# One layer on one core: a transfer of weights on ScalarE's queue placed behind a small GpSimd copy

## The chip, the cores and the metric

The kernel runs on one core of one Trainium2 chip. The metric is the device time of one execution in microseconds. The core has a matrix engine (TensorE, PE in the profile; its weight loads are PEld), a vector engine (VectorE, DVE), a scalar engine (ScalarE, ACT), GpSimd (POOL) and SyncE (SP), which only issues transfers. Transfers (DMAs) are issued by SP, ACT and POOL and moved by 16 DMA engines.

## The reference

One layer of a hybrid encoder on x of 256 rows and 2048 columns, in float32:

```
h = rms_norm(x, attn_norm)
x = x + hybrid_mixer(h, w_in, ...)      # proj = h @ w_in, two kinds of attention, then @ w_out
h = rms_norm(x, ffn_norm)
x = x + conv_ffn(h, w_up, conv_w, conv_b, w_down)
```

The projection `h @ w_in` has 6152 columns: queries, keys, values and gates of eight heads of forgetting attention, then queries, keys and values of eight heads of stick-breaking attention. The change lies in the opening, where the first 512 columns of that projection (queries of four heads) are computed and the kernel's data come in for the first time.

## The kernel before

All large products are done in two parts. A float32 operand is split into a rounded high part and a remainder (`hi`, `lo`), and three products (hi by hi, hi by lo, lo by hi) are summed in PSUM. For weights, ACT or DVE makes `hi` by a copy with a cast, and DVE makes `lo` by a subtraction. For x, TensorE transposes a block of 128 columns by a product with the identity, ACT writes `hi` (scaled by the norm's weight, `ga`), and DVE writes `lo`; both go into `hT`. The factor of the norm's root mean square is applied to the result, later.

After the opening the order is: the rest of the input projection and attention, step by step interleaved; the output projection; then the feed-forward network in parts of eight feature blocks. In those stages SP loads one 1 MB piece of weights after another, ACT and DVE split it, and TensorE multiplies.

The function `opening` (from line 383) computes the first 512 columns of the projection over the 16 blocks of x, two blocks (one "c") at a time, c from 0 to 7. Its work on PE, DVE, ACT and SP stands in the order in which it is written (`manual_schedule`); POOL's order is left to the scheduler. The pieces that matter here:

- `load_x(k, n)` (line 91): SP loads n blocks of x from block k. I call them x0, x2, x4 and so on by k.
- `load_w(c, which, queue)` (line 395): loads weights of step c, either both halves or one, on SP or on ACT. `load_w(0, 0)`, `load_w(0, 1, nc.scalar)`, `load_w(1, 0, nc.scalar)` and `load_w(1, 1)` are w00, w01, w10 and w11, 256 KB each; all four lie in one tile, w_raw.
- Lines 369 to 373: DVE clears `zeros`, POOL builds the identity in `ident` (a memset and an `affine_select`).
- `keep_busy(n)` (line 379): n products of `zeros`, whose result nobody reads. There are 14 before the first transposes and four between the transposes and the first real product.
- `columns` (line 129): TensorE turns the norm's weight from rows (`prow`) to columns (`ga`).
- `split_w(0)`: DVE casts w00 (line 407), the two blocks of x0 are transposed (139), ACT writes their `hi` (144) and DVE their `lo` (147), DVE makes w00's remainder (417); then ACT casts w01 (416) and DVE makes its remainder.
- `multiply` (line 426): four products for each half in `hi`, two in `lo`. The eight products of w00 and w01 in `hi` stand first; then, behind the preparation of step 1, the four in `lo`.
- `split_w(1)`: DVE casts w10 and w11 (line 413), the two blocks of x2 are transposed.

The start of the transfers, as written in `opening`:

```
load_x(0, 2)
nc.scalar.dma_start(prow[:KT, :], attn_norm[0].rearrange("(n p) -> n p", p=P))
act.preload_act_table_set("natural_log_exp_and_others")
load_w(0, 0)
load_w(0, 1, nc.scalar)
load_x(2, 2)
load_w(1, 0, nc.scalar)
load_w(1, 1)
load_x(4, 2)
load_w(2)
```

The layer that records the program adds the waits between engines. For transfers of SP and ACT it has eight semaphores, used in turn; a transfer that takes a semaphore again is issued only when that semaphore's former transfer has landed, and the engine that issues it waits for that.

Of the kernel before, what the change touches and what calls it, by code (L numbers as in the profile page):

```python
# [45 lines left out]
def hybrid_layer(  # L46
# [19 lines left out]
    nc = tc.nc  # L66
# [11 lines left out]
    def f32(t):  # L78
        return t.bitcast(F32)
# [10 lines left out]
    def load_x(k, n):  # L90
        nc.sync.dma_start(x2[:, :, k * P : (k + n) * P], xp[:, :, k * P : (k + n) * P])

    ident = cs[:, C_ID : C_ID + P]
# [33 lines left out]
    def columns(dst, rows, n):  # L127
        pp = psb.tile([P, 512], F32, name="pp", tag="t")
        nc.tensor.transpose(pp[:, :n], rows, ident[:n, :n])
        dve.tensor_copy(dst, pp[:, :n])  # L130
# [3 lines left out]
    def transposed_split(k, g, n=2):  # L134

        ps = psb.tile([P, 2, S], F32, name="ps_x", tag="t")
        for j in range(n):
            for t in range(NT):
                nc.tensor.transpose(
                    ps[:, j, t * P : (t + 1) * P], xt[t][:, (k + j) * P : (k + j + 1) * P], ident  # L140
                )
        for j in range(n):
            i = k + j
            act.activation(hT[:, i, 0, :], ps[:, j, :], AF.Identity, scale=g[:, i : i + 1])
        for j in range(n):
            i = k + j
            dve.scalar_tensor_tensor(
                hT[:, i, 1, :], ps[:, j, :], g[:, i : i + 1], f32(hT[:, i, 0, :]),
                op0=ALU.mult, op1=ALU.subtract,
            )  # L150

    def sums_of_squares(ss, c, tiles=range(NT)):

        for t in tiles:
            junk = late.tile([P, 512], F32, name="junk", tag="raw", bufs=4)
            act.activation(junk, xt[t][:, c * 512 : (c + 1) * 512], AF.Square, accum_out=ss[:, t, c : c + 1])
# [62 lines left out]
    def rows_of(w, k0, n, c0, cols):  # L219
        return w[k0 * P : (k0 + n) * P, c0 : c0 + cols].rearrange("(k p) c -> p k c", p=P)  # L220
# [14 lines left out]
    def of_half(h, part, t):  # L235
        return h[:, part, t * P : (t + 1) * P]
# [48 lines left out]
    with ExitStack() as actx:  # L285
# [57 lines left out]
        def attended(po, h, g, group):  # L343
# [28 lines left out]
            ident, ident, pattern=[[-1, P]], base=0, channel_multiplier=1,  # L372
# [4 lines left out]
        def keep_busy(n):  # L377
            for _ in range(n):
                nc.tensor.matmul(idle, zeros[:, :P], zeros, start=True, stop=True)
# [3 lines left out]
        def opening():  # L383

            acc = psa.tile([P, NT, 512], F32, name="acc", tag="acc")
            pairs = [[(0, 1), (1, 1)]] + [[(0, 2)]] * 7
            raws, parts = [], []

            def load_w(c, which=None, queue=nc.sync):

                if c == len(raws):
                    raw = wraw.tile([P, 2048], F32, name="w_raw", tag="w_raw")
                    raws.extend([raw[:, :1024], raw[:, 1024:]])
                for i, n in [(which, 1)] if which is not None else [(0, 2)]:
                    queue.dma_start(
                        raws[c][:, i * 512 : (i + n) * 512].rearrange("p (a b) -> p a b", a=n),
                        rows_of(wi, 2 * c + i, n, 0, 512),
                    )

            def split_w(c):  # L400
                hi = whi.tile([P, 2048], F32R, name="w_hi", tag="w_hi")
                lo = wlo.tile([P, 2048], F32R, name="w_lo", tag="w_lo")
                parts.append([t[:, :1024].rearrange("p (a b) -> p a b", a=2) for t in (hi, lo)])
                for i, n in pairs[c]:
                    cols = slice(i * 512, (i + n) * 512)
                    if c == i == 0:
                        dve.tensor_copy(hi[:, cols], raws[c][:, cols])
                        for k in range(2):
                            transposed_split(k, ga, 1)
                    elif c == 1:  # L410
                        for j in range(2):
                            half = slice(512 * j, 512 * (j + 1))
                            dve.tensor_copy(hi[:, half], raws[c][:, half])
                        transposed_split(2, ga)
                    else:
                        act.copy(hi[:, cols], raws[c][:, cols])
                    dve.tensor_tensor(
                        lo[:, cols], raws[c][:, cols], f32(hi[:, cols]), op=ALU.subtract
                    )

            def multiply(c, i, n, high):
                hi, lo = (p[:, i : i + n] for p in parts[c])
                order = [(j, l, hi) for j in range(n) for l in range(2)] if high else [(j, 0, lo) for j in range(n)]
                for m, (j, l, r) in enumerate(order):
                    for t in range(NT):
                        nc.tensor.matmul(
                            acc[:, t, :], of_half(hT[:, 2 * c + i + j], l, t), r[:, j, :],
                            start=high and c == i == m == 0, stop=not high and c == 7 and m == n - 1,
                        )

            load_x(0, 2)
            nc.scalar.dma_start(prow[:KT, :], attn_norm[0].rearrange("(n p) -> n p", p=P))
            act.preload_act_table_set("natural_log_exp_and_others")
            load_w(0, 0)
            load_w(0, 1, nc.scalar)
            load_x(2, 2)
            load_w(1, 0, nc.scalar)
# [3 lines that stand above are left out]
            load_x(6, 2)  # L441
            load_w(3)
            load_x(8, 4)
            load_w(4)
            load_x(12, 4)
            load_w(5)
            keep_busy(14)
            columns(ga, prow[:KT, :], KT)
            split_w(0)
            keep_busy(4)  # L450

            def behind(c):
                if c:
                    transposed_split(2 * c + 2, ga)
                split_w(c + 1)

            multiply(0, 0, 1, True)
            multiply(0, 1, 1, True)
            behind(0)
            sums_of_squares(ss1, 0, [0])  # L460
            multiply(0, 0, 1, False)
            multiply(0, 1, 1, False)
            for c in range(1, 8):
                if c < 7:
                    behind(c)
                sums_of_squares(ss1, c // 2, [c % 2])
                if c == 2:
                    load_w(6)
                    load_w(7)
                multiply(c, 0, 2, True)  # L470
                multiply(c, 0, 2, False)
            return acc

        with tc.high_priority(offset=AHEAD), tc.manual_schedule(
            engines={mybir.EngineType.PE, mybir.EngineType.DVE, mybir.EngineType.Activation, mybir.EngineType.SP}
        ):
            acc_q0 = opening()
# [687 lines left out]
```

## Time and profile before

| | |
|---|---|
| median of 3 runs | 1104.94 us (1104.69 to 1105.36) |
| the profiled execution | 1104.87 us |
| its span, first to last instruction | 1103.1 us |
| granted clock of TensorE | 1.000 |
| TensorE with work | 1097.9 us |
| DVE, ACT, POOL with work | 876.2, 701.6, 44.4 us |
| read from memory | 242.89 MB, 222 GB/s over the span |

A row of the timeline has the start in microseconds from the span's start, the duration, the engine, the line, the operation, out<-in, and in brackets how long the engine was idle before and what ended it. An engine's name with a q (SPq, ACTq) is its sequencer, which issues a transfer. The duration of a row with xN runs from the first of the N to the end of the last. A row of the waits has who waited for whom, microseconds in total, how often, and the longest. A row of the stretches has the stretch, its length, the busy time (and count) of PE, PEld, DVE, ACT and POOL, the granted clock, the share of the DMA engines and GB/s. Products are pipelined: the next one starts before the one before it has ended.

### The profile page before, as it was taken

How to read it: one execution, taken by the hardware profiler on the slowest of the kernel's cores; microseconds unless marked ns; L12 is line 12 of the kernel's file. 1: busy time of each engine (PE TensorE's matmuls, PEld its weight loads, DVE VectorE, ACT ScalarE, POOL GpSimd, SP SyncE). 2: the span in 40 equal slices, each digit the busy share in tenths (PEclk: the TensorE clock that was granted, in tenths of full speed). 3: DMA queues.
4: the chain of work that ended last, by engine and by line, in shares of the span. 5: the costliest groups of instructions: out<-in, count | busy, mean ns of one | idle time of the engine just before them, and what ended most of it. 6: DMA issues, size and time to landing. Idle time of an engine off the chain costs nothing. (4 is left out here: it accounts for less than half of the span.)

```text
span 1103.1 us, 14847 instructions
## 1 busy us (share of the span) xinstructions
PE 1097.9 (100%) x5872; PEld 951.4 (86%) x5872; DVE 876.2 (79%) x940; ACT 701.6 (64%) x879; POOL 44.4 (4%) x46
## 2 busy tenths in 40 slices
PE   9999999999999999999999999999999999999998
PEld 7998888888888888888888888888888888888887
DVE  5755787785775677679889988889798889889896
ACT  6543565664553567667767776767676677677753
POOL 0000000000000000000000010100000010100010
PEclk9999999999999999999999999999999999999999
DMA  8776555565555396558989597986979688987985
GB/s 290 187 230 229 189 153 160 175 217 182 184 160 187 112 318 202 188 176 208 288 225 309 191 235 263 263 268 176 318 207 308 212 219 277 247 265 196 326 210 167
DMA packets 179407, 245.96 MB, mean 223 GB/s; under 512 B 4432, under 2 KB 119018, under 8 KB 179082
## 3 DMA queue, kind: packets, MB, share of 16 engines
q1 hardware_dynamic: 162458, 209.73, 58.4%
q0 software_dynamic: 16560, 34.75, 16.6%
q8 instruction: 46, 0.75, 0.3%
q10 hardware_dynamic: 320, 0.53, 0.2%
q14 instruction: 23, 0.19, 0.0%
HBM read 242.89 MB, written 2.11 MB: 222 GB/s over the span
## 5 line engine op out<-in xcount | busy, mean ns | idle before, releaser
L209 DVE TENSOR_TENSOR w_lo<-w_raw,w_hi 128x2048 fp32r<-128x2048 f32 (+1 forms) x196 | 439.7, 2246 | 148.7 <-ACT w_hi L208 148.0
L208 ACT CAST w_hi<-w_raw 128x2048 fp32r<-128x2048 f32 (+1 forms) x196 | 367.3, 1876 | 278.6 <-PE pu L257 83.4
L257 PE MATMUL pu<-hT,w_hi 128*128 128x512 f32 x1664 | 397.1, 390 | 0.0
L257 PEld LDWEIGHTS pu<-hT,w_hi 128*128 128x128 f32 x1664 | 309.4, 188 | 62.4
L264 PEld LDWEIGHTS pu<-hT,w_lo 128*128 128x128 f32 x1664 | 213.6, 191 | 8.3
L264 PE MATMUL pu<-hT,w_lo 128*128 128x256 f32 x1664 | 216.2, 283 | 0.0
L230 PE MATMUL acc<-w_hi,hT 128*128 128x512 f32 (+1 forms) x576 | 124.9, 368 | 0.0
L230 PEld LDWEIGHTS acc<-w_hi,hT 128*128 128x128 f32 x576 | 101.2, 188 | 14.1
L209 DVE TENSOR_TENSOR w_lo<-w_sum,w_hi 128x2048 fp32r<-128x2048 f32 x30 | 68.7, 2290 | 19.8 <-ACT w_hi L208 19.8
L208 ACT CAST w_hi<-w_sum 128x2048 fp32r<-128x2048 f32 x30 | 57.3, 1909 | 42.4 <-PE pu L257 36.3
L864 ACT ACTIVATE tap<-up,ccol 128x256 f32<-128x256 f32 x176 | 74.6, 495 | 0.0
L230 PE MATMUL acc<-w_lo,hT 128*128 128x512 f32 (+1 forms) x288 | 65.0, 367 | 0.0
L230 PEld LDWEIGHTS acc<-w_lo,hT 128*128 128x128 f32 x288 | 51.5, 188 | 7.4
L969 POOL DMA_DIRECT2D w_sum<-in_w_down_dram x20 | 25.7, 1285 | 796.8 <-DVE w_lo L209 786.1
L230 PE MATMUL acc<-w_hi,oT 128*128 128x512 f32 x192 | 46.0, 392 | 0.0
L230 PEld LDWEIGHTS acc<-w_hi,oT 128*128 128x128 f32 x192 | 35.7, 188 | 7.3
L230 PE MATMUL bank_a<-w_hi,s 128*128 128x512 f32 x160 | 40.1, 393 | 0.2 <-DVE x L946 0.2
L230 PE MATMUL bank_a<-w_hi,g 128*128 128x512 f32 x160 | 40.0, 392 | 0.0
L230 PE MATMUL bank_b<-w_hi,s 128*128 128x512 f32 x160 | 40.0, 392 | 0.0
L230 PEld LDWEIGHTS bank_a<-w_hi,s 128*128 128x128 f32 x160 | 28.8, 189 | 5.8 <-issue 0.6
L230 PEld LDWEIGHTS bank_a<-w_hi,g 128*128 128x128 f32 x160 | 28.9, 189 | 5.2
L230 PEld LDWEIGHTS bank_b<-w_hi,s 128*128 128x128 f32 x160 | 28.9, 189 | 5.3
(214 smaller groups left out, 1071.7 us busy)
## 6 DMA issues: line engine op xcount, KB each, us to landing
w_raw<-in_w_up_dram SPq DMA_DIRECT2D x88, 1024.0 KB, 8.0
w_raw<-in_w_down_dram SPq DMA_DIRECT2D x44, 1024.0 KB, 6.4
w_raw<-in_w_in_dram SPq DMA_DIRECT2D x36, 1024.0 KB, 5.2
w_sum<-in_w_down_dram POOLq DMA_DIRECT2D x20, 1024.0 KB, 9.7
w_raw<-in_w_out_dram SPq DMA_DIRECT2D x16, 1024.0 KB, 5.0
w_raw<-in_w_down_dram POOLq DMA_DIRECT2D x10, 1024.0 KB, 14.7
w_raw<-in_w_in_dram SPq DMA_DIRECT2D x12, 688.0 KB, 4.0
w_raw<-in_w_in_dram SPq DMA_DIRECT2D x6, 512.0 KB, 7.0
```

What stands on the lines that cost most here:

```text
L208: act.copy(hi[:, :n], raw[:, :n])
L209: dve.tensor_tensor(lo[:, :n], raw[:, :n], f32(hi[:, :n]), op=ALU.subtract)
L230: nc.tensor.matmul(o, lhs(i, l, t), r[:, i, :], start=starts and j == 0, stop=stops and j == 3 * n - 1, skip_group_check=more,)
L257: nc.tensor.matmul(acc[:, j, :], hi[:, i, j * P : (j + 1) * P], hT[:, k].rearrange("p a b -> p (a b)"), start=k == 0, stop=False,)
L264: nc.tensor.matmul(acc[:, j, S:], lo[:, i, j * P : (j + 1) * P], hT[:, k, 0, :], start=False, stop=k == KT - 1,)
L864: act.activation(taps[w][:, j, :], u[:, j, w : w + S], AF.Copy, scale=ccol[:, w, f : f + 1])
L969: nc.gpsimd.dma_start(mem[into][:, : nk * 512].rearrange("p (a b) -> p a b", a=nk), src, accum_op=ALU.add)
```

## The change

A copy on GpSimd is put ahead of `load_w(0, 1, nc.scalar)`. It writes the identity into the first 128 columns of the place that w01 will fill, so it depends on the identity, and w01's transfer must wait for it. Later the transfer overwrites what the copy wrote. Behind the split of the first weights there are two products of zeros instead of four. From there on the line numbers of the changed kernel are one higher.

```
             load_w(0, 0)
+            nc.gpsimd.tensor_copy(raws[0][:, 512:640], ident)
             load_w(0, 1, nc.scalar)
...
             keep_busy(14)
             columns(ga, prow[:KT, :], KT)
             split_w(0)
-            keep_busy(4)
+            keep_busy(2)
```

More of the change, by code (lines that the diff above doesn't have):

```diff
@@ L434, in opening @@
             load_w(0, 0)
+            nc.gpsimd.tensor_copy(raws[0][:, 512:640], ident)
             load_w(0, 1, nc.scalar)
@@ L449, in opening @@
             split_w(0)
-            keep_busy(4)
+            keep_busy(2)
             def behind(c):
```

## Prediction

> **What bounds the kernel now.** I read the engine table of the page first, then who waited for whom on TensorE, then the timeline of the first 20 us.
>
> ```profile
> span 1103.1 us, 14847 instructions
> ...
> PE 1097.9 (100%) x5872; PEld 951.4 (86%) x5872; DVE 876.2 (79%) x940; ACT 701.6 (64%) x879; POOL 44.4 (4%) x46
> ```
>
> ```profile
> PE idle L379 <- DVE zeros L369: 1.1, 1, 1.1
> PE acc L426 <- DVE w_hi L407: 0.6, 1, 0.6
> PE bank_a L230 <- DVE x L946: 0.2, 1, 0.2
> ```
>
> TensorE shows work in 1097.9 of 1103.1 us, and the list of its waits has only three entries: 1.1 us before the first product of zeros, 0.6 us before the first real product, and 0.2 us near the end. So there is no slack behind the opening that could swallow a delay, and nothing but the opening that this change could win from: what the first products lose or gain, the end loses or gains. The most there is to win is that 0.6 us.
>
> The opening itself, from the timeline (start, duration, engine; SPq and ACTq rows are DMA issues):
>
> ```profile
> 0.73 0.46 ACTq L432 DMA_DIRECT2D prow<-in_attn_norm_dram  x1
> 0.74 0.20 POOL L370 MEMSET cs<- 128x128 f32 x1 [0.29 <-POOLq L1150]
> 0.74 0.43 SPq L91 DMA_DIRECT2D x<-in_x_dram  x1
> ...
> 1.06 3.15 PE L379 MATMUL idle<-zeros 128*128 128x256 bf16 x14 [1.06 <-DVE zeros L369]
> ...
> 1.23 0.46 SPq L395 DMA_DIRECT2D w_raw<-in_w_in_dram  x1
> 1.25 0.95 ACTq L395 DMA_DIRECT2D w_raw<-in_w_in_dram  x2
> 1.33 0.28 POOL L371 TENSOR_SCALAR_AFFINE_SELECT cs<-cs 128x128 f32<-128x128 f32 x1
> 1.57 0.09 POOL L488 MEMSET go_on<- 128x1 f32 x1
> 1.74 0.43 SPq L91 DMA_DIRECT2D x<-in_x_dram  x1
> ...
> 4.01 0.51 SPq L91 DMA_DIRECT2D x<-in_x_dram  x1
> ...
> 4.77 0.84 ACT L144 ACTIVATE hT<-ps_x,ga 128x256 fp32r<-128x256 f32 x2 [2.26 <-PE ps_x L139]
> ...
> 4.91 0.60 PE L379 MATMUL idle<-zeros 128*128 128x256 bf16 x4
> ...
> 5.57 0.37 SPq L395 DMA_DIRECT2D w_raw<-in_w_in_dram  x1
> 5.58 0.43 DVE L407 CAST w_hi<-w_raw 128x512 fp32r<-128x512 f32 x1 [1.00 <-DMA w_raw<-in_w_in_dram]
> 5.77 0.62 ACT L416 CAST w_hi<-w_raw 128x512 fp32r<-128x512 f32 x1 [0.17 <-DMA w_raw<-in_w_in_dram]
> 5.92 0.87 DVE L147 SCALAR_TENSOR_TENSOR hT<-ps_x,ga,hT 128x256 fp32r<-128x256 f32 x2
> ...
> 6.15 2.08 PE L426 MATMUL acc<-w_hi,hT 128*128 128x512 f32 x8 [0.65 <-DVE w_hi L407]
> ...
> 7.85 0.37 SPq L91 DMA_DIRECT2D x<-in_x_dram  x1
> 7.91 0.42 DVE L413 CAST w_hi<-w_raw 128x512 fp32r<-128x512 f32 x1
> ...
> 8.07 0.60 PE L139 MATMUL ps_x<-cs,x 128*128 128x128 f32 x4
> ```
>
> I name the transfers by what they carry: x0, x2, x4 ... are the loads of x from column block 0, 2, 4; w00 and w01 are the two halves of the first weights, w10 and w11 those of the second. SP issues x0 (0.74), w00 (1.23), x2 (1.74), w11; ACT issues w01 and w10 (1.25 to 2.20). The reader is to see three things. The first eight products start at 6.15, because DVE casts w00 from 5.58 on, when it lands. ACT's two activations at 4.77 make the moving operand hT before that. The last four of the eight need w01, cast by ACT at 5.77, when it lands; at (8.07 - 6.15) / 8 = 0.24 us a product the fifth starts at about 7.11.
>
> **The change, part by part.** *The copy.* It stands on POOL behind the identity's select and the small memset (1.33 and 1.57), so it starts at about 1.66. No row shows a copy there; the nearest rows of the same 128x128 size take 0.20 and 0.28 us. I take 0.3, and it ends at 1.96; between 0.2 and 0.5 nothing below changes, since it isn't the last thing waited for.
>
> *The wait that comes with it.* The two transfers on ACT now come later in the planned order of issue, behind several of SP's. The recording layer gives the DMAs of SP and ACT eight semaphores in turn, in that order, and an issue waits until the semaphore's last user has landed. In the kernel before, prow, x0, w00, x2, w01, w11, w10, x4 take numbers 0 to 7, and no ACT issue waits. In the built program of the changed kernel w11, x4, w2, x6 take 4 to 7 and w3 takes 0, so that w01 gets x0's number and w10 gets x2's. Its list of ACT instructions says so:
>
> ```
> 3 L395 DMACopy w_raw_123<-in_w_in_dram 128x512 [waits DMAHW1_49,Pool_49]
> 4 L395 DMACopy w_raw_123<-in_w_in_dram 128x512 [waits DMAHW3_49]
> 5 L144 Activation hT_76<-ps_x_160,ga_75 128x256 [waits DVE_49,PE_49]
> ```
>
> So w01 waits for x0 to land, and w10 for x2 to land; and ACT's activations of hT stand behind both issues on the same engine. That such waits hold an engine back is in the trace of before: SP's issue at 4.01 is one that waits for x0's semaphore, and its issue at 7.85 one that waits for x2's, with nothing between them but one load at 5.57, which waits for w00's. I read from them that x0 is down at 4.0 and x2 at 7.8.
>
> *When x2 lands now.* With w01 and w10 held back, x0, w00 and x2 go first. The bytes of the stretches (the last two columns are the DMA engines' share and GB/s):
>
> ```profile
> 1.00:2.00 1.00, 0.94 (x5) 0.70 (x6) 0.00 (x0) 0.78 (x1) 0.62 (x3) 1.00 0.10 10
> 2.00:3.00 1.00, 1.00 (x7) 0.69 (x6) 0.00 (x0) 0.51 (x1) 0.00 (x0) 1.00 0.76 209
> 3.00:4.00 1.00, 1.00 (x6) 0.56 (x4) 0.00 (x0) 0.00 (x0) 0.00 (x0) 1.00 1.00 320
> 4.00:5.00 1.00, 1.00 (x8) 0.69 (x7) 0.17 (x1) 0.23 (x1) 0.00 (x0) 1.00 0.96 301
> ```
>
> 10 + 209 + 320 + 301 make 840 thousand bytes started by 5.0; three loads of 262 and prow's 8 are 794, started by 4.85. Before, the first three loads (x0, w00, w01) were down by 5.77, when ACT's cast starts. I take 5.8 for x2, with 5.3 and 7.8 (no gain over before) as ends.
>
> *ACT after that.* One issue takes 0.95 / 2 = 0.47 us: 5.8 to 6.3. The activations then run from 6.3 to 7.15 instead of 4.77 to 5.61. The first product goes from 6.15 to about 6.9 (6.3 + 0.42 for one activation + some 0.15, the time from the cast's end at 6.01 to the product at 6.15), although w00 now lands some 0.7 us earlier (539 thousand bytes by 4.0 are prow, x0 and w00; with the 0.9 from 4.85 to 5.77 they are down at 4.9). That gain is covered: it waits for hT.
>
> *w01.* Issued at 4.0 instead of 1.25. x0, issued into an idle queue, took 4.0 - 0.74 = 3.3 us until it was down; by that row w01 lands at 7.3. On ACT's queue, beside SP's full one, w10 was down by 7.91 and w01 by 5.77, 2.1 us apart; with the first packet some 1.1 us after the issue (x0 is issued at 0.74, and the stretch up to 2.0 moved 10 thousand bytes) and some 0.3 until the last of it is down, that makes 7.5. I take 7.4. Ends: 6.5, and 8.5 (4.0 plus the 4.5 us that it took before). ACT is free at 7.15, so the cast runs from 7.42 to 8.04, and the fifth product starts at 8.04 + 0.15 = 8.19 instead of 7.11: **1.08 us later**. This, not the first product, sets the path: the later gap swallows the earlier one.
>
> The Trainium skill, DMA: Bandwidth & Descriptors (Latency and other measured facts), gives about 0.6 us from issue to first byte on this path; the trace puts it nearer to 1.1. By the page w01 would land at 6.9, ACT would be the later one, and the sum would be 0.8 us instead of 1.1.
>
> *What may be late next.* DVE's cast of w10 was at 7.91. w10, now issued at 5.8 behind w01 on ACT's queue, lands 2.1 us after it, at about 9.5. The products of the second weights start then:
>
> ```profile
> 9.58 0.88 DVE L147 SCALAR_TENSOR_TENSOR hT<-ps_x,ga,hT 128x256 fp32r<-128x256 f32 x2 [0.61 <-ACT hT L144]
> ...
> 9.80 2.10 PE L426 MATMUL acc<-w_hi,hT 128*128 128x512 f32 x8
> ```
>
> They are due at 9.80 + 1.08 = 10.88. The two casts of 0.43 from 9.5 end at 10.36, and the hT correction, due at 9.58 + 1.08 = 10.66, follows in time. The cover is 0.3 us; w10 later than 9.8 would add its excess.
>
> *Two products of zeros fewer.* At 0.11 to 0.15 us each (four in 0.60) they end at about 5.3 instead of 5.5. TensorE waits behind them before (0.65) and after, so they bring nothing; the wait grows to 1.6 us.
>
> *The rest.* One transpose of parameters moves by one product on TensorE, and one tiny DVE operation moves behind a reduction; nothing. SP issues some loads earlier, into a queue that is full anyway. That the delay isn't made up later is seen in the pace:
>
> ```profile
> 13.04 2.09 PE L426 MATMUL acc<-w_hi,hT 128*128 128x512 f32 x8
> ...
> 16.23 2.10 PE L426 MATMUL acc<-w_hi,hT 128*128 128x512 f32 x8
> ```
>
> A round of two blocks takes 3.19 us, and the waits above show no idle TensorE in it: the pace is TensorE's own.
>
> **Sum.** 1104.87 (the profiled execution; span 1103.1 and 1.8 around it) + 1.08 = 1105.9. The median of the runs, 1104.94, is the same within 0.1. That is 0.09%, under the 0.2% (2.2 us) which a measurement of this kernel can tell from no change.
>
> **The rivals.**
>
> *w01 comes early, or a part is made up* (+0.0 to +0.5: 1104.9 to 1105.4). With x2 down at 5.3, hT ends at 6.65 and, if w01 were down by then, the cast at 7.27 and the fifth product at 7.4: +0.3. For it: fewer transfers compete. Against it: w01 shares its time with w11 and x4.
>
> *The change only does what its words say*: ACT waits for the copy alone, until 1.96, and everything that follows on ACT keeps its place, w01 landing 0 to 0.7 us later and w00 up to 0.7 earlier. The first product could then start at 5.4 (hT's first activation ends near 5.2, 4.77 + 0.42), and the gap of 0.65 would shrink: 1104.3 to 1104.9. Against it: the list of waits.
>
> *The clock falls* (slower by more than can be missed). The zeros raise the rate of TensorE: 14 of them in 3.15 us, 0.22 each, then four in 0.60. The row of granted clock says 1.00 for all stretches, but the products double their pace at about 4.1, after 3 us of work. Now TensorE idles from 5.3 to 6.9 and again for parts of a microsecond until 8.2, some 2 us in all. If that is enough to lower the rate, the next 3 us of products go at half pace and lose 1.5 us: 1.08 + 1.5 = +2.6, 1107.5. It decides from the point at which idle time within one such 3 us stretch weighs more than work. Against it: before, 0.65 idle did nothing, and even now no 3 us are without products. The Trainium skill, TensorE: Matmul & The Clock Gate (What's actually happening), has the clock halve after at least one idle window of about 3.4 us; by that rule 1.6 us would not lower it, and the sum stays 1.1.
>
> *x2 lands as late as before*, at 7.8: issue, two activations, cast and 0.15 make 7.8 + 0.47 + 0.84 + 0.62 + 0.15 = 9.9 for the fifth product, +2.8: 1107.7. Against it: what held it up was w01 and w10.
>
> **How the numbers follow.** The forecast (+0.5 to +1.7) 0.76; early or made up 0.09; as the words say 0.04; the clock 0.06; x2 late 0.05. The likeliest time is 1105.9. The forecast's own range is 1105.4 to 1106.6; with one neighbouring case on the low side and the tail of w01 (8.5, +2.2) on the high side the range is 1105.1 to 1107.0. Slower by over 0.2% takes the last two cases, with a little less than all of them: 0.10. Faster by over 0.2% would need more than the 0.65 us there is: 0.01. Within 0.2%: 0.89.
>
> **What would show it.** In the profile of the changed kernel: ACT's issues of w01 at about 4.0 and of w10 at about 5.8, instead of both by 2.2; the first activation at 6.3; DVE's cast of w00 earlier, near 4.9; TensorE's first product at 6.9, and a second wait for ACT's cast of w01 that ends at 8.2; the transposes of 8.07 at 9.15; and from there on the same pace, with everything about 1.1 us later. If ACT issues w01 at 2.0, the reading of the semaphores is wrong; if the first 2 us of products are spaced by 0.43 instead of 0.24, the clock fell; if the opening is 1.1 us late and the end isn't, the claim that nothing swallows it is wrong.

## The result, and the profile after

The changed kernel takes 1112.21 us (median of 5, 1111.22 to 1112.74) against 1104.94: 7.3 us or 0.65% slower, ratio 1.0065 with a 95% interval of 1.0053 to 1.0076. The profiled execution took 1112.28, span 1110.5. Two executions in the experiments below, of 2839 and 5977 us, stand far from all others of their kernels and are left out of the medians and ratios. The prediction was 1105.9, range 1105.1 to 1107.0: the sign was right, the size was off by a factor of seven, and the time lies outside the range.

TensorE and what it waited for in the changed kernel (the second fence from the list of waits):

```profile
span 1110.5 us, 14843 instructions
...
PE 1101.7 (99%) x5870; PEld 953.9 (86%) x5870; DVE 876.2 (79%) x940; ACT 701.1 (63%) x879; POOL 44.6 (4%) x47
```

```profile
PE acc L426 <- ACT hT L144: 2.1, 1, 2.1
PE acc L426 <- ACT w_hi L416: 1.9, 1, 1.9
PE idle L379 <- DVE zeros L369: 1.1, 1, 1.1
PE bank_a L230 <- ACT w_hi L208: 0.5, 1, 0.5
```

The 0.6 us for DVE's cast is gone; two waits for ACT of 2.1 and 1.9 us stand in its place, one for hT and one for w01's cast. The timeline of the changed kernel's opening:

```profile
1.68 0.29 POOL L435 COPY w_raw<-cs 128x128 f32<-128x128 f32 x1
1.74 0.43 SPq L91 DMA_DIRECT2D x<-in_x_dram  x1
2.21 0.47 SPq L395 DMA_DIRECT2D w_raw<-in_w_in_dram  x1
2.71 0.43 SPq L91 DMA_DIRECT2D x<-in_x_dram  x1
3.19 0.47 SPq L395 DMA_DIRECT2D w_raw<-in_w_in_dram  x1
3.70 0.47 SPq L91 DMA_DIRECT2D x<-in_x_dram  x1
4.13 3.26 ACTq L395 DMA_DIRECT2D w_raw<-in_w_in_dram  x2
...
4.79 0.43 DVE L407 CAST w_hi<-w_raw 128x512 fp32r<-128x512 f32 x1
...
7.49 0.84 ACT L144 ACTIVATE hT<-ps_x,ga 128x256 fp32r<-128x256 f32 x2 [4.99 <-DMA x<-in_x_dram]
...
8.02 2.08 PE L426 MATMUL acc<-w_hi,hT 128*128 128x512 f32 x4 [2.10 <-ACT hT L144]
...
11.33 0.62 ACT L416 CAST w_hi<-w_raw 128x512 fp32r<-128x512 f32 x1 [3.00 <-DMA w_raw<-in_w_in_dram]
...
12.00 2.08 PE L426 MATMUL acc<-w_hi,hT 128*128 128x512 f32 x4 [1.90 <-ACT w_hi L416]
```

The copy ends at 1.97, but ACT issues w01 only at 4.13, and its second issue, w10, ends at 4.13 + 3.26 = 7.39: it waited for x2. The first product starts at 8.02 instead of 6.15. w01 lands at 11.33, 7.2 us after its issue, and the fifth product starts at 12.00 instead of 7.11. Later rows of the same view:

```profile
13.88 1.05 PE L139 MATMUL ps_x<-cs,x 128*128 128x128 f32 x4
14.58 2.06 PE L426 MATMUL acc<-w_lo,hT 128*128 128x512 f32 x4
16.44 0.85 PE L139 MATMUL ps_x<-cs,x 128*128 128x128 f32 x4
17.04 2.09 PE L426 MATMUL acc<-w_hi,hT 128*128 128x512 f32 x8
...
20.23 2.10 PE L426 MATMUL acc<-w_hi,hT 128*128 128x512 f32 x8
```

Two things are to be seen. Four products take 2.06 to 2.08 us at 8.02, 12.00 and 14.58, and eight take 2.09 at 17.04: until about 17 TensorE ran at half pace. And the products of the second weights start 7.24 later than before (17.04 against 9.80), those of the third 7.19 later (20.23 against 13.04). So the whole 7.2 us arises ahead of 17 us: 4.9 until the fifth product, and 2.35 between it and the second weights (5.04 us there, 2.69 before). Another 0.2 comes at the end, where the wait for ACT's cast is 0.5 us and before one of 0.2 stood; the chain there hangs on a late transfer in both kernels, and that part was not followed up.

### The profile page after: what moved, and what is told of

Read it like the earlier page. It is cut to its first block, busy times and chain, and to the rows that moved or that the text cites. A ratio compares the mean times of both kernels' runs of the same rounds, so it can differ in the third digit from the quotient of the medians.

```text
span 1110.5 us, 14843 instructions
## 1 busy us (share of the span) xinstructions
PE 1101.7 (99%) x5870; PEld 953.9 (86%) x5870; DVE 876.2 (79%) x940; ACT 701.1 (63%) x879; POOL 44.6 (4%) x47
```

## The experiments

The theory after the result had three parts: the shared semaphores hold w01 back to 4.1; a transfer lands behind whatever either queue has issued before it, so that w01 then lands late; and the waits that follow keep TensorE's clock down. The second part turned out too strict, as is said below. The rivals were that ACT's second wait is the cause, that ACT's queue is served badly, that GpSimd's wait costs by itself, and that the two zeros do. The kernel before, run beside these on other chips, took 1105.49, 1105.38 and 1105.45 us (medians), so each run is compared with its own.

**Each half alone.** The first run takes the zeros away and has no copy:

```
-            keep_busy(4)
+            keep_busy(2)
```

> The kernel before with two products of zeros fewer ahead of the first product and no copy. Theory (the cost is the two late transfers on ACT's queue, and the clock only falls because of the waits that they make): nothing to measure, 1104.7 to 1105.4. Rival (the two zeros hold the clock up): the first products at 0.43 us apart instead of 0.24, 1106.5 or more.

It took 1105.33 against 1105.49, ratio 0.9999 (0.9990 to 1.0008): no difference. The second has the copy, and `keep_busy(4)`.

> The changed kernel with the four products of zeros of before, so the copy alone. Theory: like the changed kernel, 1111.2 to 1112.7, w01 issued near 4.1 and landing near 11.3, the fifth product near 12.0. Rival (the missing zeros cost the part of the 7.3 us that is the slow clock, some 2.3 us): 1109.5 to 1110.2.

It took 1112.03, ratio 1.0061 (1.0046 to 1.0076), with the fifth product at 11.70: the copy alone makes the loss.

**The clock.** The run with the copy alone shows the granted clock (the column before the last two) in the stretches of its opening:

```profile
6.40:9.80 3.40, 1.25 (x4) 0.59 (x4) 1.48 (x3) 0.84 (x2) 0.00 (x0) 1.00 1.00 334
9.80:16.60 6.80, 4.90 (x15) 3.92 (x16) 2.52 (x6) 2.06 (x5) 0.00 (x0) 0.50 1.04 389
16.60:20.00 3.40, 3.40 (x20) 2.83 (x18) 2.99 (x4) 2.40 (x5) 0.00 (x0) 0.99 0.58 155
```

It fell after a stretch in which TensorE worked 1.25 of 3.4 us, and took 6.8 us to come back. To keep it up, two runs fill the waits of the changed kernel with products of zeros, the first with 10 and 8, the second with 14 and 24:

```
-            keep_busy(2)
+            keep_busy(14)
...
             multiply(0, 0, 1, True)
+            keep_busy(24)
             multiply(0, 1, 1, True)
```

> The changed kernel with ten products of zeros instead of two ahead of the first product, and eight more between the fourth and the fifth, so that TensorE works through its two waits. Theory: first and fifth product start near 8.0 and 12.0 as in the changed kernel, but the clock is up by then, products 0.24 us apart, and the end is some 2 us earlier: 1109.5 to 1110.5. Rival (all of the 7.3 us is the late landing): 1111.2 to 1112.7.

1111.46, ratio 1.0053 (1.0037 to 1.0070): in the rival's range. It doesn't settle the question, for the clock didn't stay up: eight zeros at the higher pace end 2.1 us before the fifth product, and the trace shows the clock falling again. The second:

> The changed kernel with 14 products of zeros instead of two ahead of the first product, and 24 between the fourth and the fifth. Theory (some 2.3 us of the 7.3 are the slow clock behind the waits): the clock, once up, stays up through both waits, the products behind them are 0.24 us apart, 1109.3 to 1110.6. Rival (the clock costs nothing beside the landing): 1111.2 to 1112.7.

```profile
7.02 1.17 PE L426 MATMUL acc<-w_hi,hT 128*128 128x512 f32 x4
8.03 2.79 PE L379 MATMUL idle<-zeros 128*128 128x256 bf16 x24
11.87 1.19 PE L426 MATMUL acc<-w_hi,hT 128*128 128x512 f32 x4 [1.04 <-ACT w_hi L416]
```

1110.85, ratio 1.0044 (1.0030 to 1.0057), between the theory's range and the rival's. Its timeline has the fifth product at 11.87, hardly earlier than in the changed kernel (12.00), but the four take 1.19 instead of 2.08. Of the 5.4 us that are left, 4.8 are there when the second weights start (14.62 against 9.80): that is the late landing. The rest was not traced. The clock is worth 1.1 (against the copy alone) to 2.35 us (in the two traces).

**ACT's second wait.** Here w10 goes to SP, so that ACT waits once. In this build w01 waits for w00's semaphore instead of x0's, and is issued at 4.99 instead of 4.13:

```
-            load_w(1, 0, nc.scalar)
+            load_w(1, 0)
```

> The changed kernel with w10 issued by SP, so that ACT waits once, for w01, and not a second time for x2 ahead of its activations. In the built program w01 now waits for w00's semaphore. Theory (transfers land in the order of their issue over both queues; w01 is the one that sets the path): the first product moves up to some 5.9, but w01, issued near 4.8 behind even more of SP's loads, lands at 11 to 13, and the time is no better than the changed kernel's, 1111 to 1114. Rival (ACT's second wait, for x2, is the cause): the 2.5 us by which the activations come earlier are won, 1109 to 1110.

```profile
4.99 0.36 ACTq L395 DMA_DIRECT2D w_raw<-in_w_in_dram  x1
...
5.98 1.25 PE L426 MATMUL acc<-w_hi,hT 128*128 128x512 f32 x4
...
11.71 0.62 ACT L416 CAST w_hi<-w_raw 128x512 fp32r<-128x512 f32 x1 [5.42 <-DMA w_raw<-in_w_in_dram]
```

The first product starts at 5.98, 2.0 us earlier than in the changed kernel, and the time is 1113.30, ratio 1.0070 (1.0056 to 1.0084). The early first product wins nothing: the fifth still waits for w01, which lands at 11.7 here and sets the path.

**The place in the order of issue.** This kernel has nothing of the change: SP issues w01 and w10 behind x6, ACT waits for nothing.

```
-            load_w(0, 1, nc.scalar)
...
-            load_w(1, 0, nc.scalar)
...
             load_x(6, 2)
+            load_w(0, 1)
+            load_w(1, 0)
             load_w(3)
```

> The kernel before with w01 and w10 issued by SP directly behind x6, near 4.2 and 4.7, as late as w01 in the changed kernel; no copy, no wait on ACT, four products of zeros. Theory (the place in the order of issue is what costs): w01 lands near 10.5 to 12, the first product is early (5.3 to 6.2), the fifth at 11.2 to 12.7, and the time is 1110.5 to 1113.5, although nothing of the change is in the kernel but the late place. Rival (ACT's own queue or its wait is what costs): SP's w01 lands by 9 and the time stays under 1109.5.

```profile
4.22 2.05 SPq L395 DMA_DIRECT2D w_raw<-in_w_in_dram  x3
...
11.32 0.62 ACT L416 CAST w_hi<-w_raw 128x512 fp32r<-128x512 f32 x1 [5.32 <-DMA w_raw<-in_w_in_dram]
```

1111.94, ratio 1.0053 (1.0039 to 1.0067), with w01 down at 11.32 as in the changed kernel (11.33). The first product starts early, at 5.99, and the fifth at 11.99. A late place in the order alone makes a loss of this size; neither ACT's queue nor a wait on it is needed.

**The wait without the shared semaphore.** Two memsets in w01's place instead of the copy end at 1.87, about when the copy ends, and in this build w01 and w10 keep the semaphores of the kernel before.

```
-            nc.gpsimd.tensor_copy(raws[0][:, 512:640], ident)
+            for _ in range(2):
+                nc.gpsimd.memset(raws[0][:, 512:1024], 0.0)
```

> The changed kernel with two memsets of 128x512 on GpSimd into the place of w01 in place of the copy behind the identity (the output is the same, the transfer overwrites them). In the built program w01 and w10 keep the semaphores of the kernel before, and w01 waits for GpSimd alone, so that it is issued near 2. Theory (the semaphores shared with x0 and x2 cost the time, not the wait for GpSimd): 1104.3 to 1105.6, w10 issued near 2.5. Rival (any wait behind GpSimd puts the weights behind the other loads): 1109 or more.

```profile
1.74 0.43 SPq L91 DMA_DIRECT2D x<-in_x_dram  x1
1.90 0.84 ACTq L395 DMA_DIRECT2D w_raw<-in_w_in_dram  x2
...
8.70 0.62 ACT L416 CAST w_hi<-w_raw 128x512 fp32r<-128x512 f32 x1 [2.70 <-DMA w_raw<-in_w_in_dram]
...
9.46 0.37 SPq L91 DMA_DIRECT2D x<-in_x_dram  x1
```

It missed: 1107.40, ratio 1.0024 (1.0014 to 1.0033), between the theory and the rival. w01, issued 0.16 us behind x2 instead of ahead of it, lands at 8.70, and x2 itself at 9.45. Its nine executions fall into two groups, five of 1106.81 to 1107.40 with a mean granted clock of 1.000 and four of 1108.75 to 1109.50 with 0.998; the profiled one is the slowest of the four. One memset less puts the issue back ahead of x2:

> The run with two memsets with one of them left out, so that w01 is issued near 1.35, ahead of x2 (1.74) as in the kernel before, and w10 near 1.85, just behind x2. Theory (the place in the order of issue is what costs): w01 lands by 6.0, within 0.3 us of the kernel before, 1104.8 to 1105.8. Rival (a wait on GpSimd, or two zeros fewer beside it, costs by itself what the two memsets showed): 1107 or more.

w01 is issued at 1.29 and lands by 5.7; 1105.89 against 1105.45, ratio 1.0001 (0.9993 to 1.0010). So neither a wait on GpSimd as such (here it holds the issue up by 0.04 us) nor the zeros cost; 0.6 us more of waiting, past x2's issue, costs 1.9 by the medians or 2.6 by the ratio, each against the kernel before.

**Fewer loads ahead of w01.** In two runs x4 and what follows on SP wait, by a further copy on GpSimd, for x0:

```
+            nc.gpsimd.tensor_copy(x2[:, 0, 4 * P : 5 * P], x2[:, 0, :P])
             load_x(4, 2)
```

> The changed kernel with a further copy on GpSimd, from x0's first block into the place of x4, ahead of x4's load, so that SP's loads from x4 on are issued only after x0 has landed, together with w01. Theory (landing in order of issue): w01, still issued near 4.5, has only w11 and x4 before it and lands at 8 to 9 instead of 11.3; the fifth product near 9.3, and 1107.5 to 1110. Rival (a transfer issued by ACT takes some 7 us here whatever stands before it): it lands at 11 or later, 1111 or more.

1113.13, ratio 1.0068 (1.0055 to 1.0082). The build moved the loads of parameters ahead, w01 got the semaphore of one of them and was issued only at 6.58; it landed at 11.25, after 4.7 us instead of 7.2. Its numbers lie in the rival's range, but the late issue alone can put them there, so it didn't test what it was for. In the second the parameters stay in their place:

> The idea of the run with SP held back, with the loads of parameters kept in their place behind the weights (there the build had moved them ahead, and w01 waited for one of them): x4's load waits for a copy on GpSimd that reads x0, so that x4 and w01 are issued together, near 4.4 to 4.8, and w2 and the rest behind them. Theory (what SP has issued before stands ahead of w01): only x2, w11 and x4 are ahead, w01 lands at 7.3 to 8.5 instead of 11.3, fifth product 8.1 to 9.3, 1106.3 to 1109.0. Rival (a transfer issued by ACT at this time takes 6 us or more whatever stands ahead of it): 1110.5 or more.

```profile
4.31 0.38 SPq L91 DMA_DIRECT2D x<-in_x_dram  x1
...
4.55 0.84 ACTq L396 DMA_DIRECT2D w_raw<-in_w_in_dram  x2
...
10.71 0.62 ACT L417 CAST w_hi<-w_raw 128x512 fp32r<-128x512 f32 x1 [4.38 <-DMA w_raw<-in_w_in_dram]
```

1111.74, ratio 1.0047 (1.0031 to 1.0063): a miss by the theory's numbers, and in the rival's range, since w01 is issued at 4.55 and takes 6.1 us. It isn't ACT's queue, for the same load issued by SP at 4.22 took 7.1; whether the loads ahead of it matter is seen only in its parts. A transfer is done when 16 parts have landed, one from each DMA engine, and the trace has the time of each. The eighth part of w01 came at 8.34 here and at 10.21 in the changed kernel, as the order of issue has it; the last came at 10.69, because the last three engines ran 1.4 to 2.4 us behind the eighth. So fewer loads ahead brought half of w01 earlier, but not its end. With two memsets, too, the eighth part came at 6.06 against 5.15 with one, and the last at 8.68 against 5.68: the order explains the smaller part of that delay, and late engines the larger.

**A better order.** All on SP, w01 directly behind w00, without a copy, with four and with two products of zeros:

```
-            load_w(0, 1, nc.scalar)
+            load_w(0, 1)
...
-            load_w(1, 0, nc.scalar)
+            load_w(1, 0)
```

> The kernel before with w01 and w10 issued by SP, w01 directly behind w00 and w10 behind x2, no copy, four products of zeros. Theory (landing in order of issue): w00 lands alone, near 4.8 instead of 5.6, w01 near 5.8, the first product starts near 5.6 instead of 6.15: 1104.2 to 1104.8. Rival (transfers on two queues share the engines, and one queue alone moves less): w01 or w10 later than before, 1105.2 to 1106.

> The kernel before with w01 and w10 issued by SP and two products of zeros instead of four. Theory: TensorE is free 0.2 us earlier, and only if w00 has been cast by then: 1104.0 to 1104.8, within 0.3 of the run with four. Rival (the clock): slower by 1 or more than the run with four.

1105.63 against 1105.38, ratio 0.9999 (0.9990 to 1.0008), and 1106.24, ratio 1.0007 (0.9998 to 1.0016): the theory missed both. With four zeros 15 parts of w01 are there at 5.64, but the last comes at 6.83. With two zeros the first product starts at 5.41, but the last of w01 lands at 6.42 instead of 5.75, and the fifth product starts at 7.12, as before (7.11): what the first product wins is lost again at w01. No order that was tried beats the kernel before.

## Why the prediction was wrong

**The step that failed: when w01 lands.** The prediction read ACT's queue as served beside SP's, 2.1 us a transfer, and put w01 at 7.4; it landed at 11.33. Its rows held the other reading: the loads were issued in the order x0, w00, w01, w10, x2 and came down in that order, at 4.0, 5.58, 5.77, before 7.91, and 7.85. Counted so, what stands ahead of an issue at 4.13 is what SP has issued by then: x0, w00, x2, w11, x4 and x6 of 262 thousand bytes and w2 of 524, with prow's 8 some 2100. The stretches of the changed kernel:

```profile
3.00:4.00 1.00, 1.00 (x6) 0.56 (x4) 0.00 (x0) 0.00 (x0) 0.00 (x0) 1.00 0.90 303
4.00:5.00 1.00, 1.00 (x6) 0.76 (x5) 0.39 (x2) 0.00 (x0) 0.00 (x0) 1.00 1.00 297
5.00:6.00 1.00, 0.92 (x5) 0.37 (x3) 0.21 (x1) 0.00 (x0) 0.00 (x0) 1.00 0.83 244
6.00:7.00 1.00, 0.00 (x0) 0.00 (x0) 0.00 (x0) 0.00 (x0) 0.00 (x0) 1.00 1.04 322
```

The 303 thousand of the first of them and 231 before it had been moved by 4.0, so about 1570 were ahead; at some 300 GB/s that is 5.2 us, plus 0.9 for w01 itself: 10.1. Its eighth part came at 10.21 and its last at 11.31: the 1.2 us that the count lacks lie in the late parts. The queues' rows (q1 is SP's queue, q10 ACT's) fit: between 4.2 and 7.4, after w01's issue, only SP's queue moved anything, and from 7.4 to 11.4 both did.

```profile
DMA packets 740, 0.96 MB, mean 302 GB/s; under 512 B 50, under 2 KB 488, under 8 KB 740
## 3 DMA queue, kind: packets, MB, share of 16 engines
q1 hardware_dynamic: 740, 0.96, 97.3%
```

```profile
q1 hardware_dynamic: 685, 1.05, 73.4%
q10 hardware_dynamic: 171, 0.32, 28.7%
```

So the count fits w01, but the order is not a strict one. By their last parts w01 (issued at 4.13) landed ahead of x6, which SP had issued at 3.70, at 11.31 against 11.81; and w10, issued by ACT at 7.06, landed at 13.39, ahead of x8, which SP had issued at 4.93 (15.03). ACT's transfer got nothing for 3.5 us (its first packet came at 7.6) and then shared the engines with SP's; what decides when the sharing starts was not tried.

The same error made the upper end of the range too low: 8.5 took over the 4.5 us of the kernel before, where w01 had been the third in line.

**The shared semaphores** were read rightly: ACT's issues at 4.13 and behind x2, the activations held up behind both. So was that the later gap swallows the earlier one: moving the first product by 2 us (w10 on SP) won nothing. x2 was put at 5.8 and came at 7.04; 15 of its 16 parts were there by 5.46, in keeping with the estimate, and one engine was late.

**The clock** stood among the rivals, with 0.06, against the forecast's 0.76. Its condition, that idle time outweighs work within one stretch, fits the traces; the prediction weighed it with some 2 us of idle time in all, and the two waits made 4.0. With waits of 2 us each TensorE worked 1.25 of 3.4 us in the run with the copy alone, and the clock fell; in the changed kernel's profile it didn't rise before 16.9, so the slow products there are a late rise and not a fall. The price, put at 1.5, was 1.1 to 2.35. The page's rule that the prediction set beside it, a fall after at least one idle window (the Trainium skill, TensorE: Matmul & The Clock Gate, What's actually happening), reads too mildly here: in the run with the copy alone it fell, and no stretch of that length was idle.

**The rival that the change only does what its words say** was priced at 1104.3 to 1104.9. Tried with two memsets, it is 1107.40. The shared semaphores make up some 4 to 5 of the 6.5 to 7.3 us; the rest is lost even without them, when w01 is issued behind x2.

**The two products of zeros** cost and bring nothing that could be measured, as forecast. **That nothing is made up later** held: 7.24 at the second weights, 7.19 at the third, and 7.4 at the end.

What stays open is why one or a few of the 16 engines run far behind in some openings. Between the eighth and the last part of one of the first loads lay up to 1.8 us in the changed kernel and 3.6 with two memsets, and at most 1.0 in the kernel before and with one memset. It was not tried by itself.

## What to carry to other kernels

Before delaying a transfer, count what the other queues will have issued by then: here w01 waited for most of those bytes, on ACT's queue as on SP's, and a delay of 0.6 us past one large load cost about 2. After adding a wait, read the built program for the semaphores: a wait moves transfers in the planned order, and the transfer may inherit a semaphore whose last user is still in flight. Waits of 2 us on TensorE in the opening cost its clock as well here, so such a wait is priced at more than its length.

## What the runs showed of the hardware

The first transfers of SP's and ACT's queues (x0, w00, w01, w10 and x2 in the kernel before, the last two issued within 0.01 us) came down in about the order in which they were issued over both; in the changed kernel a later issue of ACT passed an earlier one of SP (w10 at 7.06 and 13.39, x8 at 4.93 and 15.03). The granted clock changed in steps of one length: in the run with the copy alone the trace has it up at 6.41, down at 9.82 and up at 16.65, with two memsets up at 5.78, down at 9.19 and up at 12.60, which are 3.41 us or twice that. It fell after stretches of that length with 1.25 us of TensorE's work (the copy alone), 1.34 (10 and 8 zeros) and 1.40 (w10 on SP), and stayed up through one with 2.38 (14 and 24 zeros, 9.27 to 12.69). Its first rise came at 4.05 in the kernel before and at 16.94 in the changed one, and with one memset at 10.12, although TensorE had worked in the same way until 4.2; that execution took 1107.12, the fastest of the same kernel 1105.15.
